# Where the even and odd tokens are told apart: in the split of the MLP activations, or in the weight load of the up-projection

## The chip, the cores and the metric

The program runs on one core of a Trainium2 chip. The metric is device microseconds of one execution. Beside the time there is a profile of one execution: for each engine the start and duration of its instructions, and what it waited for. TensorE appears twice in it, as PE (the matmuls) and as PEld (the loads of the stationary operand, which run beside the matmuls).

## The reference, cut to what matters

Two decoder layers act on 256 tokens of width 2048, all in float32. In each layer four groups of attention heads are followed by an output projection, and then comes the gated MLP, with which this document is concerned:

```
h = rms_norm(x, ffn_norm)                  # 256 x 2048
u = causal_depthwise_conv(h @ w_up, ...)   # w_up: 2048 x 11264, width 3 along the tokens
gate, val = split(u, 2)
x = x + (silu(gate) * val) @ w_down        # w_down: 5632 x 2048
```

## The kernel before

**Precision by three products.** Every float32 operand of the large products is split into a high and a low part in the type float32r (`hi`, `lo`), and the product is made of three matmuls: high by high, low by high, high by low (lines 269, 270 and 271 in `Gemm.steps`). The activations are the stationary operand, 128 rows by 128 tokens; the weights are the moving one, 128 rows by 512 columns. Each of the three matmuls has its own load of the stationary operand, since the operand alternates between high and low.

**Tokens.** The 256 tokens are two halves, `t` = 0 and 1, each with an accumulator in PSUM of 128 partitions by 512 columns. For most products half `t` holds tokens 128t to 128t + 127. The up-projection is different: half 0 holds the even tokens and half 1 the odd ones. What follows it (`turn`, line 845 and after) transposes 32 by 32 blocks of the two halves, interleaves them in pairs, and writes them to DRAM and back, so that the channels come to lie on the partitions and the tokens in order along the row, as the convolution needs them.

**How the order is made before.** `x_ready` transposes the residual `xs` in blocks of 128 by 128 on TensorE (line 208, tiles `tr_f` ahead of the MLP and `tr_n` ahead of the next layer) and splits each 128 by 256 block into `hTs` with `split_T`: ScalarE writes the high part (line 190), VectorE the low part (line 191). For the MLP, `even_odd` makes these two instructions read the PSUM block with a step of two elements, and `halves` names the halves of the written row. So `hTs` holds 128 even tokens and then 128 odd ones, and the stationary operand of `up` is 128 neighbouring elements per partition, as for every other product. `hTs` has for each of the 16 row blocks `k` a row of 256 float32r elements for the high part and another for the low part.

**Order of the work.** The loop over the up-projection makes 11 pairs of a gate product and a value product of 512 columns in each layer, in three groups of 3, 4 and 4, each followed by its part of the down-projection. The weights come by DMA from the SyncE queue, 1 MB at a time, and ScalarE and VectorE split them (lines 242 and 243). Side work (transposes, convolution, splits) is put between the matmul steps by a queue of generators (`Task`, `tick`). The order of instructions on each engine is fixed when the program is built. The attention part has products with fewer columns and products in plain float32, which the program issues as two TensorE instructions each.

Of the kernel before, what the change touches and what calls it, by code (L numbers as in the profile page):

```python
# [19 lines left out]
P = 128  # L20
NT = 2
SEQ = 256
DM = 2048
KT = DM // P
# [50 lines left out]
def tile_trunk(ctx: ExitStack, tc: tile.TileContext, x, xT, pvec, rows, ctab,  # L75
# [35 lines left out]
    class Task:  # L111
        def __init__(self, gen, q=queue):
            self.gen, self.done = gen, False
            q.append(self)
# [4 lines left out]
    def tick(n=1):  # L119
        for _ in range(n):  # L120
            for task in [*movers, *list(queue)[:1]]:
                with tc.issue_after(last_mm[0].ins):
                    try:
                        next(task.gen)
                    except StopIteration:
                        task.done = True
                        (movers if task in movers else queue).remove(task)
# [19 lines left out]
    def pcol(l, n, i=0):  # L147
        o = l * PVW + PV[n] + i
        return pv[:, o:o + 1]
# [14 lines left out]
    hTs = big.tile([P, KT, 2, SEQ], F32R, name="hTs")  # L164
# [8 lines left out]
    def psum(name):  # L173
        return trp.tile([P, 512], F32, tag="tr", name=name)
# [14 lines left out]
    def split_T(src, gain, hi, lo):  # L189
        nc.scalar.activation(hi, src, AF.Identity, scale=gain)  # L190
        nc.vector.scalar_tensor_tensor(lo, src, gain, hi.bitcast(F32), op0=ALU.mult, op1=ALU.subtract)

    def even_odd(a):

        return a.rearrange("p (m t) -> p t m", t=NT)

    def halves(a):
        return a.rearrange("p (t m) -> p t m", t=NT)

    def transpose_split(src, n, cnt, gain, kt0, dh, dl, eo=False):  # L200

        for j0 in range(0, cnt, 2):
            if j0:
                yield
            ps = psum(f"tr_{n}_{j0}")
            for j in (j0, j0 + 1):
                for t in range(NT):
                    nc.tensor.transpose(ps[:, (j - j0) * SEQ + t * P:(j - j0) * SEQ + (t + 1) * P],
                                        src[:, t, j * P:(j + 1) * P], ident)
            for j in (j0, j0 + 1):  # L210
                a, h, lo = ps[:, (j - j0) * SEQ:(j - j0 + 1) * SEQ], dh[:, kt0 + j, :], dl[:, kt0 + j, :]
                if eo:
                    a, h, lo = even_odd(a), halves(h), halves(lo)
                split_T(a, gain(j), h, lo)

    def acc_bank(name):
        return accp.tile([P, 512], F32, tag="acc", name=name)
# [8 lines left out]
    def split_weights(src, k, N, n, nk):  # L226


        if k % 4 == 0 and (n, k) not in loaded:
            load_weights(src, k, n, nk)  # L230
        raw = loaded[n, k - k % 4][:, k % 4:k % 4 + 2]
        if n == "dq0" and k == 0:
            src(raw, 0, 1, nc.scalar)
            src(raw[:, 1:], 1, 1)
        elif n == "dq0" and k < 8:
            src(raw, k, 2)
        hi, lo = [], []
        for s in ((0, 1), (1, 2)) if n == "dq0" and k == 0 else ((0, 2),):
            r = raw[:, s[0]:s[1], :N]
            h, w = (wspl.tile([P, 2, 512], F32R, tag=p, name=f"{p}_{n}_{k + s[0]}")[:, :s[1] - s[0], :N]  # L240
                    for p in ("hi", "lo"))
            nc.scalar.copy(h, r)  # L242
            nc.vector.tensor_tensor(w, r, h.bitcast(F32), op=ALU.subtract)  # L243
            hi += [h[:, i] for i in range(s[1] - s[0])]
            lo += [w[:, i] for i in range(s[1] - s[0])]
        return hi, lo

    class Gemm:


        def __init__(self, n, N, act, wsrc, nk, bank=acc_bank):
            self.n, self.N, self.act, self.wsrc, self.nk = n, N, act, wsrc, nk
            self.acc = [bank(f"acc_{n}_{t}") for t in range(NT)]
            self.done = 0

        def steps(self, k0, cnt):
            N = self.N
            for g0 in range(k0, k0 + cnt, 2):
                hi, lo = split_weights(self.wsrc, g0, N, self.n, self.nk)
                parts = [(*self.act(g0 + i), hi[i], lo[i]) for i in range(2)]  # L260
                order = [(t, i) for t in range(NT) for i in range(2)]
                if self.n == "dq0" and g0 == 0:
                    order = [(t, i) for i in range(2) for t in range(NT)]
                for t, i in order:
                    o = self.acc[t][:, :N]
                    ah, al, wh, wl_ = parts[i]
                    first, last = self.done + i == 0, self.done + i == self.nk - 1
                    sh, sl = ah[:, t * P:(t + 1) * P], al[:, t * P:(t + 1) * P]
                    nc.tensor.matmul(o, sh, wh, start=first, stop=False)  # L269
                    nc.tensor.matmul(o, sl, wh, start=False, stop=False)  # L270
                    last_mm[0] = nc.tensor.matmul(o, sh, wl_, start=False, stop=last)  # L271
                self.done += 2
                tick(rate[0])
# [5 lines left out]
    def wchunk(w, k0=0):  # L279

        def src(raw, k, cnt, q=nc.sync):
            q.dma_start(raw[:, :cnt, :w.shape[2]], w[:, k0 + k:k0 + k + cnt, :])
        return src
# [7 lines left out]
    def slotted(slots, tasks):  # L291
        def get(k):
            finish(tasks[k // 4])
            hi, lo = slots[k // 4]
            return hi[:, k % 4, :], lo[:, k % 4, :]
        return get

    def evac(acc, n, N, rs, tag, bufs):
        d = tmp.tile([P, NT, 512], F32, tag=tag, name=f"{tag}_{n}", bufs=bufs)
        for t in range(NT):  # L300
            nc.scalar.activation(d[:, t, :N], acc[t][:, :N], AF.Identity, scale=rs[:, t:t + 1])
        return d
# [12 lines left out]
    def x_ready(c, n, gname, l, ssq, r, reo=None):  # L315

        yield from transpose_split(xs[:, :, c * 512:(c + 1) * 512], f"{n}_{c}", 4,
                                   lambda j: pcol(l, gname, 4 * c + j), 4 * c, hTs[:, :, 0], hTs[:, :, 1],
                                   reo is not None)
        yield  # L320
        yield from x_stats(c, n, ssq, r, reo)

    def x_stats(c, n, ssq, r, reo=None):
        for t in range(NT):
            tc.keep_in_program_order(sumsq(xs[:, t, c * 512:(c + 1) * 512], f"{n}_{c}_{t}", ssq[:, t, c:c + 1]))
        if c == 3:
            yield
            s = sml.tile([P, NT], F32, tag="xs_s", name=f"s_{n}")
            nc.vector.tensor_reduce(s, ssq, axis=AX.X, op=ALU.add)
            if n[0] == "n":  # L330
                with tc.issue_after(tc.keep_in_program_order(nc.scalar.preload_act_table_set(LNEXP)).ins):
                    rsqrt(r, s, f"x{n}", 1.0 / DM, NT)
            else:
                rsqrt(r, s, f"x{n}", 1.0 / DM, NT)
            if reo is not None:
                rd = dram.tile([SEQ], F32, tag="rd", name=f"rd_{n}")
                nc.gpsimd.dma_start(rd.rearrange("(t p) -> p t", p=P), r)
                nc.gpsimd.dma_start(reo, rd.rearrange("(p t) -> p t", t=NT))
# [137 lines left out]
    for l in range(L):  # L476
# [46 lines left out]
        def cq_task(l=l):  # L523
            for t in range(NT):
                sumsq(cq[:, t, :], f"cq{l}_{t}", ss_lat[:, 2 + t:3 + t])
            rsqrt(r_lat[:, 2:4], ss_lat[:, 2:4], f"cq{l}", 1.0 / QR, 2)
            yield from transpose_split(cq, f"cq{l}", 4, lambda j: pcol(l, "cq", j), 0, *cqT)
# [3 lines left out]
        acc = lat_gemm.acc  # L531
# [72 lines left out]
        for c, (c0, wu) in enumerate(((0, w_uqn[l]), (GW, w_uqr[l]))):  # L604
            w = wu.shape[2]
            acc = Gemm(f"uq{l}_{c}", w, slotted([cqT], [t_cq]), wchunk(wu), 4).run()
# [4 lines left out]
        for c in range(2):  # L611
            acc = Gemm(f"ukv{l}_{c}", 512, slotted([ckvT], [t_lat]), wchunk(w_ukv[l, c]), 2).run()
# [217 lines left out]
        reo = sml.tile([P, NT], F32, tag="reo", name=f"reo_{l}", bufs=1)  # L830

        def post_out(c, acc):
            add_x(c, acc)
            h_task[c] = Task(x_ready(c, f"f{l}", "ffn", l, ssq_x, rf, reo))
# [21 lines left out]

        def up(n, j):

            acc = Gemm(f"up_{n}", 512, hT, wchunk(w_up[l, j]), KT).run()
            u = evac(acc, n, 512, reo, "v", 1)  # L860
            d = tmp.tile([P, 4, SEQ], F32, tag="qk", name=f"u_{n}", bufs=2)
            gen = turn(u, d, n)
            next(gen)
            return d, Task(gen, movers)
# [39 lines left out]
        for ti, (j0, j1) in enumerate(THIRDS):  # L904
            act, tasks = [], []
# [23 lines left out]
            nk = (j1 - j0) * 4  # L929
# [74 lines left out]
```

## Time and profile before

| | |
|---|---|
| median of 3 runs | 2226.51 us (2224.54 to 2228.56) |
| the profiled execution | 2224.77 us, of which the span from first to last instruction is 2222.6 us |
| PE busy | 2215.8 us, 10196 matmuls |
| PEld busy | 1839.2 us, 10196 loads |
| VectorE, ScalarE busy | 1452.1 us, 1192.0 us |
| granted TensorE clock, mean | 0.999 of full speed |

[...] The rate is read from the distance of one start to the next.

### The profile page before, as it was taken

To read this page: it belongs to the slowest core of one execution; us is meant where nothing else is said; L and a number is where in the kernel's file an instruction comes from. 1 tells how busy PE (TensorE), PEld (TensorE's weight loads), DVE (VectorE), ACT (ScalarE), POOL (GpSimd) and SP (SyncE) were. 2 spreads that over 40 slices of the span, in tenths; PEclk is the share of its full clock that TensorE was granted. 3 is DMA by queue.
4 is the path that set the end of the run, shared out by engine and by line. 5 is a ranking of instruction groups with operands and counts; after the bars stand their busy time and mean duration, and the time that the engine had idled before them with its cause. 6 is when DMAs were issued, how large, how long until landed. Compare 5 with 4: busy or idle time off the path is not lost.

```text
span 2222.6 us, 27073 instructions
## 1 busy us (share of the span) xinstructions
PE 2215.8 (100%) x10196; PEld 1839.2 (83%) x10196; DVE 1452.1 (65%) x2071; ACT 1192.0 (54%) x1651; POOL 3.9 (0%) x11
## 2 busy tenths in 40 slices
PE   9999999999999999999999999999999999999999
PEld 8888888888888888888888888888888888888887
DVE  6865865667566664667568658665766676656664
ACT  7555545555446553555556555455554555435552
POOL 0000000000000000000000000000000000000000
PEclk9999999999999999999999999999999999999999
DMA  8535445777677865777555444457775778658774
GB/s 323 199 133 171 155 156 185 216 238 242 212 213 242 252 217 195 235 238 234 183 171 195 146 155 168 152 190 220 234 245 199 230 237 243 212 197 243 232 234 150
DMA packets 163988, 460.84 MB, mean 207 GB/s; under 512 B 100496, under 2 KB 106000, under 8 KB 115728
## 3 DMA queue, kind: packets, MB, share of 16 engines
q1 hardware_dynamic: 63744, 411.63, 55.0%
q10 hardware_dynamic: 99984, 47.46, 9.3%
q8 instruction: 80, 1.31, 0.2%
q14 instruction: 52, 0.43, 0.1%
q0 software_dynamic: 128, 0.00, 0.0%
HBM read 433.89 MB, written 25.17 MB: 207 GB/s over the span
## 4 chain that ended last, share of the span: by engine, by line
PE 99%; DVE 0%; DMA 0%; ACT 0%; issue 0%; SPq 0%; DVEq 0%; ACTq 0%
PE acc_dn L270 7%; PE acc_dn L269 7%; PE acc_up_g L271 7%; PE acc_dn L271 7%; PE acc_up_g L269 7%; PE acc_up_v L269 7%; PE acc_up_g L270 7%; PE acc_up_v L270 7%; PE acc_up_v L271 7%; PE acc_out L271 3%; PE acc_out L269 3%; PE acc_out L270 3%; PE acc_aq L269 1%; PE acc_bk L271 1%; PE acc_av L269 1%; PE acc_bk L269 1%
## 5 line engine op out<-in xcount | busy, mean ns | idle before, releaser
L243 DVE TENSOR_TENSOR lo_dn<-raw_dn,hi_dn 128x1024 fp32r<-128x1024 f32 x176 | 214.9, 1224 | 163.6 <-ACT hi_dn L242 163.6
L243 DVE TENSOR_TENSOR lo_up_g<-raw_up_g,hi_up_g 128x1024 fp32r<-128x1024 f32 x176 | 213.1, 1220 | 163.4 <-ACT hi_up_g L242 163.4
L242 ACT CAST hi_dn<-raw_dn 128x1024 fp32r<-128x1024 f32 x176 | 185.8, 1056 | 230.0 <-PE acc_dn L270 200.8
L242 ACT CAST hi_up_g<-raw_up_g 128x1024 fp32r<-128x1024 f32 x176 | 185.2, 1055 | 201.4 <-PE acc_up_v L270 66.4
L243 DVE TENSOR_TENSOR lo_up_v<-raw_up_v,hi_up_v 128x1024 fp32r<-128x1024 f32 x176 | 213.6, 1223 | 117.0 <-ACT hi_up_v L242 117.0
L242 ACT CAST hi_up_v<-raw_up_v 128x1024 fp32r<-128x1024 f32 x176 | 185.1, 1053 | 184.3 <-PE acc_up_v L270 80.9
L269 PE MATMUL acc_up_g<-hi_up_g,hTs 128*128 128x512 f32 x704 | 274.2, 390 | 0.0
L271 PE MATMUL acc_up_g<-lo_up_g,hTs 128*128 128x512 f32 x704 | 273.9, 389 | 0.0
L270 PE MATMUL acc_up_g<-hi_up_g,hTs 128*128 128x512 f32 x704 | 273.9, 389 | 0.0
L269 PE MATMUL acc_up_v<-hi_up_v,hTs 128*128 128x512 f32 x704 | 273.9, 389 | 0.0
L270 PE MATMUL acc_up_v<-hi_up_v,hTs 128*128 128x512 f32 x704 | 273.9, 389 | 0.0
L271 PE MATMUL acc_up_v<-lo_up_v,hTs 128*128 128x512 f32 x704 | 273.9, 389 | 0.0
L271 PEld LDWEIGHTS acc_up_g<-lo_up_g,hTs 128*128 128x128 f32 x704 | 132.2, 188 | 27.5
L271 PEld LDWEIGHTS acc_up_v<-lo_up_v,hTs 128*128 128x128 f32 x704 | 132.2, 188 | 27.5
L269 PEld LDWEIGHTS acc_up_v<-hi_up_v,hTs 128*128 128x128 f32 x704 | 132.2, 188 | 27.4
L270 PEld LDWEIGHTS acc_up_v<-hi_up_v,hTs 128*128 128x128 f32 x704 | 132.2, 188 | 27.4
L270 PEld LDWEIGHTS acc_up_g<-hi_up_g,hTs 128*128 128x128 f32 x704 | 132.2, 188 | 27.3
L269 PEld LDWEIGHTS acc_up_g<-hi_up_g,hTs 128*128 128x128 f32 x704 | 132.2, 188 | 27.3
L243 DVE TENSOR_TENSOR lo_out<-raw_out,hi_out 128x1024 fp32r<-128x1024 f32 x64 | 78.3, 1224 | 57.0 <-ACT hi_out L242 54.1
L242 ACT CAST hi_out<-raw_out 128x1024 fp32r<-128x1024 f32 x64 | 67.3, 1051 | 63.0 <-PE acc_out L270 46.5
L269 PE MATMUL acc_dn<-hi_dn,a0h_f 128*128 128x512 f32 x192 | 74.9, 390 | 0.0
L269 PE MATMUL acc_dn<-hi_dn,a1h_f 128*128 128x512 f32 x192 | 74.8, 389 | 0.0
(576 smaller groups left out, 4535.7 us busy)
## 6 DMA issues: line engine op xcount, KB each, us to landing
raw_up_g<-in_w_up_dram SPq DMA_DIRECT2D x88, 1024.0 KB, 5.2
raw_up_v<-in_w_up_dram SPq DMA_DIRECT2D x88, 1024.0 KB, 5.2
raw_dn<-in_w_down_dram SPq DMA_DIRECT2D x88, 1024.0 KB, 4.9
raw_out<-in_w_out_dram SPq DMA_DIRECT2D x32, 1024.0 KB, 4.8
td_g<-T_g ACTq DMA_DIRECT2D x22, 512.0 KB, 2.6
u_g<-td_g ACTq DMA_DIRECT2D x88, 128.0 KB, 6.0
td_v<-T_v ACTq DMA_DIRECT2D x22, 512.0 KB, 2.8
u_v<-td_v ACTq DMA_DIRECT2D x88, 128.0 KB, 5.8
```

The lines of the kernel that those rows point to most:

```text
L242: nc.scalar.copy(h, r)
L243: nc.vector.tensor_tensor(w, r, h.bitcast(F32), op=ALU.subtract)
L269: nc.tensor.matmul(o, sh, wh, start=first, stop=False)
L270: nc.tensor.matmul(o, sl, wh, start=False, stop=False)
L271: last_mm[0] = nc.tensor.matmul(o, sh, wl_, start=False, stop=last)
```

## The change

The split of the MLP activations writes `hTs` in token order, with both operands read and written in sequence, as for the other products. `Gemm` has a new flag `eo`, which only `up` sets. With it, the stationary operand of half `t` is the columns t, t + 2, t + 4, ... of the 256: 128 elements per partition, 8 bytes apart. What each accumulator receives is the same as before. No instruction is added, removed or moved; the access patterns of the splits and of the up-projection's weight loads are others.

```
-                a, h, lo = ps[:, (j - j0) * SEQ:(j - j0 + 1) * SEQ], dh[:, kt0 + j, :], dl[:, kt0 + j, :]
-                if eo:
-                    a, h, lo = even_odd(a), halves(h), halves(lo)
-                split_T(a, gain(j), h, lo)
+                split_T(ps[:, (j - j0) * SEQ:(j - j0 + 1) * SEQ], gain(j), dh[:, kt0 + j, :], dl[:, kt0 + j, :])
...
-        def __init__(self, n, N, act, wsrc, nk, bank=acc_bank):
+        def __init__(self, n, N, act, wsrc, nk, bank=acc_bank, eo=False):
+            self.eo = eo
...
-                    sh, sl = ah[:, t * P:(t + 1) * P], al[:, t * P:(t + 1) * P]
+                    cols = slice(t, SEQ, NT) if self.eo else slice(t * P, (t + 1) * P)
+                    sh, sl = ah[:, cols], al[:, cols]
...
-            acc = Gemm(f"up_{n}", 512, hT, wchunk(w_up[l, j]), KT).run()
+            acc = Gemm(f"up_{n}", 512, hT, wchunk(w_up[l, j]), KT, eo=True).run()
```

## Rows read from the trace of the kernel before

**Rows 1.** The page: busy time, share of the span and instructions of each engine.
```profile
PE 2215.8 (100%) x10196; PEld 1839.2 (83%) x10196; DVE 1452.1 (65%) x2071; ACT 1192.0 (54%) x1651; POOL 3.9 (0%) x11
```

**Rows 2.** The page: chain that ended last, share of the span by engine.
```profile
PE 99%; DVE 0%; DMA 0%; ACT 0%; issue 0%; SPq 0%; DVEq 0%; ACTq 0%
```

**Rows 3.** Waits of PE (all three) and the longest of PEld: total us, times, longest.
```profile
PE wps L105 <- DVE warm L102: 1.1, 1, 1.1
PE acc_dq L269 <- ACT hi_dq L242: 0.5, 1, 0.5
PE tr_yc L208 <- DVE y_c L432: 0.4, 2, 0.2
...
PEld pT_a L404 <- ACT lg_a L396: 2.3, 8, 0.4
```

**Rows 4.** Stretch of up-projection: us, busy PE, PEld, DVE, ACT, POOL; PEclk, DMA, GB/s.
```profile
420.00:540.00 120.00, 120.00 (x531) 99.41 (x530) 79.13 (x102) 68.27 (x84) 0.00 (x0) 1.00 0.81 251
```

**Rows 5.** Groups by form: up-projection matmuls and loads, count | busy, mean ns | idle.
```profile
L270 PE MATMUL acc_up_g<-hi_up_g,hTs 128*128 128x512 f32 x704 | 273.9, 389 | 0.0
...
L270 PEld LDWEIGHTS acc_up_g<-hi_up_g,hTs 128*128 128x128 f32 x704 | 132.2, 188 | 27.3
```

**Rows 6.** Timeline of the up-projection: start us, duration us, instruction.
```profile
391.58 0.39 PE L269 MATMUL acc_up_g<-hi_up_g,hTs 128*128 128x512 f32 x1
391.58 0.19 PEld L270 LDWEIGHTS acc_up_g<-hi_up_g,hTs 128*128 128x128 f32 x1
391.81 0.39 PE L270 MATMUL acc_up_g<-hi_up_g,hTs 128*128 128x512 f32 x1
391.81 0.19 PEld L271 LDWEIGHTS acc_up_g<-lo_up_g,hTs 128*128 128x128 f32 x1
...
393.62 0.39 PE L269 MATMUL acc_up_g<-hi_up_g,hTs 128*128 128x512 f32 x1
```

**Rows 7.** Timeline, float32r products with 256 columns, first and last of 18 matmuls.
```profile
73.93 0.28 PE L269 MATMUL acc_uq<-hi_uq,a0h_cq 128*128 128x256 f32 x1
...
75.97 0.28 PE L271 MATMUL acc_uq<-lo_uq,a0h_cq 128*128 128x256 f32 x1
```

**Rows 8.** Timeline, float32r products with 324 columns, first and last of 13 matmuls.
```profile
29.92 0.31 PE L269 MATMUL acc_lat<-hi_lat,hTs 128*128 128x324 f32 x1
...
31.71 0.32 PE L269 MATMUL acc_lat<-hi_lat,hTs 128*128 128x324 f32 x1
```

**Rows 9.** Timeline, plain float32 products with 128 and 256 columns, and 4 columns.
```profile
110.56 0.38 PE L418 MATMUL s_d<-dT_d 128*128 128x128 f32 x2
110.78 0.39 PE L418 MATMUL s_d<-dTr_d,qz 128*128 128x128 f32 x2
111.00 0.60 PE L420 MATMUL s_d<-dT_d 128*128 128x256 f32 x2
111.44 0.59 PE L420 MATMUL s_d<-dTr_d,qz 128*128 128x256 f32 x2
111.87 0.27 PE L645 MATMUL qk_d<-ident,a2l_dq 128*128 128x128 f32 x1
...
58.14 0.36 PE L561 MATMUL cum<-fz,ct 128*128 128x4 f32 x2
58.36 0.36 PE L562 MATMUL cum<-fz,ct 128*128 128x4 f32 x2
58.59 0.48 PE L269 MATMUL acc_aq<-hi_aq,hTs 128*128 128x512 f32 x1
```

**Rows 10.** The splits by line: duration ns min/median/max, first and last start us.
```profile
L190 ACT ACTIVATE hTs<-tr_f,pv x32: 463/474/477, 343.4 to 1507.5; 128x256 fp32r<-128x256 f32 x32
L190 ACT ACTIVATE hTs<-tr_n,pv x16: 456/470/477, 1081.6 to 1122.2; 128x256 fp32r<-128x256 f32 x16
...
L191 DVE SCALAR_TENSOR_TENSOR hTs<-tr_f,pv,hTs x32: 476/482/489, 344.7 to 1508.0; 128x256 fp32r<-128x256 f32 x32
L191 DVE SCALAR_TENSOR_TENSOR hTs<-tr_n,pv,hTs x16: 477/482/485, 1082.9 to 1122.7; 128x256 fp32r<-128x256 f32 x16
```

More of the change, by code (lines that the diff above doesn't have):

```diff
@@ L191, in split_T, with transpose_split @@
         nc.vector.scalar_tensor_tensor(lo, src, gain, hi.bitcast(F32), op0=ALU.mult, op1=ALU.subtract)
[L193 to L200, printed above, removed]
+    def transpose_split(src, n, cnt, gain, kt0, dh, dl):
         for j0 in range(0, cnt, 2):
@@ L317, in x_ready @@
         yield from transpose_split(xs[:, :, c * 512:(c + 1) * 512], f"{n}_{c}", 4,
-                                   lambda j: pcol(l, gname, 4 * c + j), 4 * c, hTs[:, :, 0], hTs[:, :, 1],
-                                   reo is not None)
+                                   lambda j: pcol(l, gname, 4 * c + j), 4 * c, hTs[:, :, 0], hTs[:, :, 1])
         yield
```

## Prediction, made before the change was run

> **What bounds the kernel now.** I read the page first. TensorE's matmuls cover the whole span and VectorE and ScalarE about 65% and 54% of it [rows 1]; the chain of work that ended last is 99% matmuls [rows 2]. The list of waits confirms it: PE waited three times for anything, 2.0 us in all, and its weight loads at most 2.3 us for any one cause; no wait belongs to the up-projection or to `hTs` [rows 3]. So only what alters the distance from one matmul to the next can alter the time by much. [...]
>
> Then the timeline, for the rate. Line 269 starts at 391.58 and, nine matmuls later, at 393.62: 2.04 us / 9 = 226.7 ns from one to the next [rows 6]. The same timeline shows the load: the load for the next matmul starts when the current matmul starts, and lasts 188 ns in the record, so that about 39 ns of each turn have no load in them (27.3 us idle / 704) [rows 5, 6]. The reader should see two things that run side by side in each turn, the stream of 512 columns and the load of 128 for the next turn; the later of them sets the turn.
>
> **What the change removes.** The step of two in the reads of PSUM: 32 splits on ScalarE and 32 on VectorE. The same instruction on tiles of the same shape without that step is in the trace, ahead of the next layer. ScalarE takes 474 ns with the step and 470 without, VectorE 482 and 482 [rows 10]. That is 32 x 4 ns = 0.13 us on ScalarE, on an engine with half its time free and with no wait of PE behind it: worth 0. If the cover were gone it would be the 0.13 us. The number of instructions, transposes, DMAs and waits stays; nothing moves past a queue.
>
> **What it adds.** A step of two, 8 bytes, in the stationary operand of every up-projection matmul. There are six groups of 704 (three lines, gate and value) [rows 5], 4224 in all, and 4224 x 226.7 ns = 957.6 us, 43% of the time. One nanosecond per matmul is 4.2 us or 0.19%. No load in the trace has a step, so its cost must be bounded.
>
> First, how long does a load without a step occupy TensorE? The 188 ns of the record contain a latency that overlaps: where a product has only 4 columns, four pairs of load and matmul start from 58.14 to 58.59, 0.45 / 4 = 112 ns each [rows 9]. The columns are then next to nothing and the load sets the turn. For float32r the shortest turn in the trace is at 256 columns: 17 turns from 73.93 to 75.97, 120.0 ns [rows 7]. So the load takes about 112 ns and at most 120.
>
> Second, what does the stream take? Between 256 and 512 columns the turn grows from 120.0 to 226.7 ns: 106.7 / 256 = 0.417 ns per column, one cycle of 2.4 GHz. What is left is the same at both: 120.0 - 256 x 0.417 = 13.3 ns per matmul. The 324-column product agrees, with 1.79 us / 12 = 149.2 ns against 135.0 + 13.3 = 148.3 [rows 8]. In the up-projection the stream therefore sets the turn, and a load may grow from 112 or 120 ns to about 227 before it is late: by a factor of 1.9 to 2.0.
>
> Estimate of the added cost, from below and from above:
> - Load as fast as without a step, or slower by up to 1.9: hidden behind the stream, 0.
> - Load of twice 112 ns: 224 ns, still 0. Twice 120 ns: 240 ns, 13.3 ns more per turn than 226.7, 4224 x 13.3 = 56 us. This is the upper end that I use.
> - The far bound from rows: a load that can't run beside the stream at all, 4224 x 112 = 473 us. Nothing in the trace is near that; I keep it as a tail only.
> - Below nothing: the plain float32 products leave less over than float32r: 217.5 ns at 256 columns (0.87 us / 4) and 110 at 128 (0.44 / 4), so 0.84 ns per column and 110 - 107.5 = 2.5 ns [rows 9]. If the 13.3 ns belonged to how a dense float32r operand is loaded and a stepped one were loaded in the plain way, each turn would lose 10.8 ns: 4224 x 10.8 = 46 us.
>
> I take 0. The row nearest to a stepped load is that of the dense load, and it would have to become 1.9 times as long before anything is seen. ScalarE's and VectorE's reads at the same step of 8 bytes cost nothing in [rows 10], though there from PSUM and at a slower pace, so this is a weak hint.
>
> [...]
>
> **Sum.** Profiled execution 2224.77 us, of which 2222.6 us is the span and 2.2 us lies around it; minus 0.13 us that is hidden; plus 0: about 2225. The profiled execution lies 1.7 us below the median of the three runs shown, 2226.51, whose spread is 4 us. I give 2226.
>
> **Rivals.**
> - *The stationary read disturbs the moving stream (slower).* Place: the 13.3 ns that each float32r matmul takes beyond its columns. [...] A dense load covers 128 x 4 = 512 bytes per partition; with the step it spans 1024. If the excess is what the load takes from the stream and it goes with the length of the span, it doubles: 13.3 x 4224 = 56 us, 2281 us. For it: the excess is fixed per matmul, as a load is. Against it: a fixed cost of float32r that has nothing to do with the load would look the same. It decides from about 1 ns per matmul on, since there is no slack in the stream. [...] The late load of 240 ns has the same price.
> - *The load becomes far longer (slower by more).* At three times 112 ns the turn would be 336 ns, 109 ns more: 461 us, 2686 us. For it speaks only that no stepped load is on record; against it, the step is small. About 5 in 100.
> - *The excess of float32r goes (faster).* 46 us less, 2179 us, as worked out above. It needs a load path that depends on the step, and nothing in the trace shows one.
> - *The change does nothing to the loads but alters the order of instructions* because the program is built with other operand ranges: PE's waits are 2.0 us in all, so this is worth a microsecond or two either way, inside no change.
>
> **How the numbers follow.** About 0.2% of the time, 4.5 us, is what a measurement can tell from no change. Forecast, load hidden and stream undisturbed: 0.62. Slower: 0.33, of which 0.21 at up to 56 us (either mechanism, fully or in part), 0.07 between that and the tail, 0.05 in the tail. Faster: 0.05. Hence faster 0.05, same 0.62, slower 0.33. For 8 in 10 the range must take in the 56 us: from 2221 (4 us under the lowest run) to 2286 (the 2281 of the first rival and the spread of the runs). The forecast's own range is 2222 to 2231.
>
> **What would show it.** In the changed kernel line 269 of the up-projection should again start every 226.7 ns, PE's span from the first to the last of such a run be unchanged, and the splits take 470 and 482 ns. If the recorded load grows from 188 ns but the distance stays, the load was hidden. A distance of 240 ns would show the first rival or the late load; which of the two, only a product with fewer columns tells: with a late load the turn would not shrink with the columns, with a disturbed stream it would. A distance near 217 ns would be the faster rival. Other engines can't make the forecast wrong by much: in the up-projection they have a third of their time free [rows 4].

## The result, and the profile after

The changed kernel takes 2252.85 us (2252.72 to 2253.34, four runs) against 2225.8 us: a ratio of 1.0124, 95% interval 1.0112 to 1.0137, or 27 us slower. No change was forecast, at 2226; the range reached to 2286 and held the time.

The page of the changed kernel, its busy times; TensorE's matmuls still cover the span, and nothing else grew by more than 3 us against [rows 1] but the loads, by 22:
```profile
PE 2244.0 (100%) x10196; PEld 1861.3 (83%) x10196; DVE 1455.1 (65%) x2071; ACT 1190.9 (53%) x1651; POOL 3.8 (0%) x11
```

Its waits of PE, in four lines where [rows 3] had three; together 2.4 us, none in the up-projection:
```profile
PE wps L105 <- DVE warm L102: 1.1, 1, 1.1
PE acc_dq L261 <- ACT hi_dq L232: 0.6, 2, 0.4
PE tr_yc L201 <- DVE y_c L423: 0.4, 2, 0.2
PE acc_dq L263 <- DVE lo_dq L233: 0.3, 1, 0.3
```

Its stretch of up-projection, in the columns of [rows 4]: 516 matmuls in 120 us where there were 531, at the same granted clock of 1.00. Beside it the groups of [rows 5]:
```profile
420.00:540.00 120.00, 120.00 (x516) 99.27 (x515) 77.95 (x102) 67.14 (x81) 0.00 (x0) 1.00 0.78 241
```
```profile
L262 PE MATMUL acc_up_g<-hi_up_g,hTs 128*128 128x512 f32 x704 | 277.4, 394 | 0.0
...
L262 PEld LDWEIGHTS acc_up_g<-hi_up_g,hTs 128*128 128x128 f32 x704 | 135.9, 193 | 28.2
```

And its timeline, for the rate, as in [rows 6]. Each matmul lasts 0.39 us in the record and the next starts about 0.23 us after it, so they overlap and the distance of the starts is the turn; the two matmuls shown are twelve turns apart:
```profile
480.14 0.39 PE L263 MATMUL acc_up_v<-lo_up_v,hTs 128*128 128x512 f32 x1
480.14 0.19 PEld L261 LDWEIGHTS acc_up_v<-hi_up_v,hTs 128*128 128x128 f32 x1
480.38 0.19 PEld L262 LDWEIGHTS acc_up_v<-hi_up_v,hTs 128*128 128x128 f32 x1
...
482.94 0.39 PE L263 MATMUL acc_up_g<-lo_up_g,hTs 128*128 128x512 f32 x1
```

2.80 us / 12 = 233.3 ns per turn, against 226.7. So 6.6 ns x 4224 = 28 us: this is nearly the whole difference of the spans, 2251.1 - 2222.6 = 28.5 us. The order of the instructions is the same on every engine. The reader should see what doesn't fit a late load: the recorded load grew by only 5 ns, and about 40 ns of each turn still have none (28.2 us / 704). The splits run as before: 472 ns on ScalarE with the step gone (474 in [rows 10]), 480 on VectorE (482).

### The profile page after: what moved, and what is told of

Read it like the earlier page. It is cut to its first block, busy times and chain, and to the rows that moved or that the text cites. A ratio compares the mean times of both kernels' runs of the same rounds, so it can differ in the third digit from the quotient of the medians.

```text
span 2251.1 us, 27073 instructions
## 1 busy us (share of the span) xinstructions
PE 2244.0 (100%) x10196; PEld 1861.3 (83%) x10196; DVE 1455.1 (65%) x2071; ACT 1190.9 (53%) x1651; POOL 3.8 (0%) x11
## 4 chain that ended last, share of the span: by engine, by line
PE 99%; DVE 0%; DMA 0%; ACT 0%; issue 0%; SPq 0%; DVEq 0%; ACTq 0%
PE acc_up_g L261 7%; PE acc_up_v L261 7%; PE acc_up_g L263 7%; PE acc_up_g L262 7%; PE acc_up_v L262 7%; PE acc_up_v L263 7%; PE acc_dn L261 7%; PE acc_dn L263 7%; PE acc_dn L262 7%; PE acc_out L263 2%; PE acc_out L261 2%; PE acc_out L262 2%; PE acc_aq L261 1%; PE acc_bk L263 1%; PE acc_cq L263 1%; PE acc_bk L261 1%
## 5 line engine op out<-in xcount | busy, mean ns | idle before, releaser
L232 ACT CAST hi_dn<-raw_dn 128x1024 fp32r<-128x1024 f32 x176 | 185.4, 1053 | 231.0 <-PE acc_dn L262 200.5
L261 PE MATMUL acc_up_g<-hi_up_g,hTs 128*128 128x512 f32 x704 | 277.8, 395 | 0.0
L262 PE MATMUL acc_up_g<-hi_up_g,hTs 128*128 128x512 f32 x704 | 277.4, 394 | 0.0
L261 PE MATMUL acc_up_v<-hi_up_v,hTs 128*128 128x512 f32 x704 | 277.4, 394 | 0.0
L262 PE MATMUL acc_up_v<-hi_up_v,hTs 128*128 128x512 f32 x704 | 277.4, 394 | 0.0
L262 PEld LDWEIGHTS acc_up_v<-hi_up_v,hTs 128*128 128x128 f32 x704 | 135.9, 193 | 28.4
L261 PEld LDWEIGHTS acc_up_v<-hi_up_v,hTs 128*128 128x128 f32 x704 | 135.9, 193 | 28.3
L261 PEld LDWEIGHTS acc_up_g<-hi_up_g,hTs 128*128 128x128 f32 x704 | 135.9, 193 | 28.2
L262 PEld LDWEIGHTS acc_up_g<-hi_up_g,hTs 128*128 128x128 f32 x704 | 135.9, 193 | 28.2
```

## The experiments

**Which part costs.** Two kernels with one part of the change each. In the first the split stays as it was, in even and odd tokens, and only the load gets the step:
```
-                    sh, sl = ah[:, t * P:(t + 1) * P], al[:, t * P:(t + 1) * P]
+                    cols = slice(t, SEQ, NT) if self.n[:2] == 'up' else slice(t * P, (t + 1) * P)
+                    sh, sl = ah[:, cols], al[:, cols]
```


> The kernel before, with its split into even and odd tokens kept, and only the step of two put into the up-projection's weight loads; so the tokens of the MLP reach the accumulators in another order and the output leaves the right order out. Theory A or B (the loads cost all of it): 2252 to 2254 us, 233.3 ns from matmul to matmul in the up-projection. Rival (the split in token order is what costs, through the engines that feed TensorE): 2224 to 2228 us.

In the second the change is made and only the step taken out again:
```
-            acc = Gemm(f"up_{n}", 512, hT, wchunk(w_up[l, j]), KT, eo=True).run()
+            acc = Gemm(f"up_{n}", 512, hT, wchunk(w_up[l, j]), KT).run()
```


> The changed kernel with the step taken out of the weight loads: the split writes token order, the up-projection reads 128 neighbouring tokens, and the order of the tokens behind it is left out. Theory A or B: 2224 to 2228 us as before the change, 226.7 ns from matmul to matmul. Rival (the split costs): 2252 us.

Measured: 2252.78 us (ratio 1.0124, 1.0109 to 1.0139) and 2225.01 us (1.000, 0.9991 to 1.0009). The loads cost all of it, the splits nothing.

**A load that is late, or a stream that is disturbed?** A kernel that runs nothing but rows of 60 equal matmuls, back to back:
```
s, m = ops[n][:, 0, :], ops[n][:, 1, :]
...
base = off + (i % 2) * 1024
a = s[:, base:base + step * (P - 1) + 1:step]
nc.tensor.matmul(p[:, :N], a, m[:, 0:N], start=i == 0, stop=i == cnt - 1)
```


> This kernel leaves the whole computation out (it writes x back) and measures the load by itself: runs of 60 matmuls whose stationary operand is 128 elements with a step of 1, 2, 3, 4 or 8, with 512, 384, 256, 128 and 32 moving columns in float32r, and some in plain float32 and bfloat16. What is read is the distance from one matmul to the next. All theories: 226.7 ns for step 1 at 512 columns, 120 at 256. Theory A (the stepped load takes time from the moving stream, or adds a fixed piece to each turn): about 233.3 ns for step 2 at 512 columns, and the same 6.6 ns on top at 384 and 256 columns (180, 127). Theory B (the load itself becomes long and is late): about 233 ns at step 2 whatever the columns, 512, 384 or 256, and at 32 columns too. Within A: if the cost goes with the span of bytes that is read, step 3 costs 13 and step 4 costs 20 ns more than step 1; if it is the same for any step, 6.6 ns for all. An odd first element makes no difference in either.

Its timeline, the first matmul of some of the rows; each row is 60 matmuls long, so the distance to the next row's first, over 60, is the turn. In the names, "two" is the step, and a, b, c, d are 512, 384, 256 and 128 columns:
```profile
39.58 0.39 PE L40 MATMUL r_two_a<-sr 128*128 128x512 f32 x1
53.58 0.39 PE L40 MATMUL r_twoodd_a<-sr 128*128 128x512 f32 x1
67.58 0.40 PE L40 MATMUL r_three_a<-sr 128*128 128x512 f32 x1
81.71 0.40 PE L40 MATMUL r_four_a<-sr 128*128 128x512 f32 x1
95.81 0.41 PE L40 MATMUL r_eight_a<-sr 128*128 128x512 f32 x1
...
110.53 0.33 PE L40 MATMUL r_one_b<-sr 128*128 128x384 f32 x1
120.95 0.34 PE L40 MATMUL r_two_b<-sr 128*128 128x384 f32 x1
131.35 0.40 PE L40 MATMUL r_four_b<-sr 128*128 128x384 f32 x1
145.35 0.28 PE L40 MATMUL r_one_c<-sr 128*128 128x256 f32 x1
152.54 0.28 PE L40 MATMUL r_two_c<-sr 128*128 128x256 f32 x1
159.74 0.39 PE L40 MATMUL r_four_c<-sr 128*128 128x256 f32 x1
173.74 0.22 PE L40 MATMUL r_one_d<-sr 128*128 128x128 f32 x1
180.39 0.28 PE L40 MATMUL r_two_d<-sr 128*128 128x128 f32 x1
187.45 0.39 PE L40 MATMUL r_four_d<-sr 128*128 128x128 f32 x1
```

| turn, ns | 512 columns | 384 | 256 | 128 |
|---|---|---|---|---|
| step 1 | 226.7 (mean from the eleventh start on) | 173.7 | 119.8 | 110.8 |
| step 2 | 233.3 | 173.3 | 120.0 | 117.7 |
| step 4 | 235.0 | 233.3 | 233.3 | 233.6 (see below) |

Both theories fall. At 384 and 256 columns the step of two costs nothing, so there is no fixed piece per turn (theory A) and no load of 230 ns (theory B). At 128 columns the load sets the turn: 111 ns without a step, 118 with a step of two, where 128 columns at 0.417 ns are 53. The step of four shows what a late load looks like: 233 ns at 384 and 256 columns alike. Theory A's price by the span falls too: steps of three and eight took 235.5 and 245.3 ns at 512 columns, where 13 ns more had been expected for three and 20 for four. Thus the load of the changed kernel takes about 118 ns (an estimate, from the row with 128 columns), far from late, and still the turn at 512 columns is 6.6 ns longer. (The granted clock was 1.00 from 180.39 to 187.45 us, the row of step two and 128 columns, and 0.50 from 201.47 to 214.23; it fell within the row of step four between them, and the rows with 32 columns behind it are left aside.) In bfloat16 no cost was seen at 512 columns: 216 ns without a step, 215.8 at steps of two, four and eight.

The load alone moved the turn at 512 columns from 226.7 to 233.3 ns without being late; so the running matmuls are not free of it.

**The same in the whole kernel.** A step of four, over the high and the low row of `hTs` together, and the halving of the columns, with dense and with stepped loads:
```
+            row = hTs[:, k, :, :].rearrange("p a s -> p (a s)")
+            return row[:, t:2 * SEQ:4], row[:, t + 2:2 * SEQ:4]
...
+                    for c in (slice(0, 256), slice(256, 512)) if self.n[:2] == "up" else (slice(0, N),):
+                        nc.tensor.matmul(o[:, c], sh, wh[:, c], start=first and not c.start, stop=False)
```


> The changed kernel with a step of four in the up-projection's loads, taken from the high and the low row of hTs together, so the product is of mixed-up operands: the right tokens and parts are left out. The first probe's row for step 4: the load sets the turn at 233.3 ns for 384, 256 and 128 columns, and at 512 columns the turn is 235.0. If that holds in the kernel, 226.7 becomes 235.0: 2224.8 + 4224 x 8.3 ns = 2260 us. Theory A as first put, cost by the span of bytes read: three times 6.6 ns, 2309 us.

> The kernel before, each up-projection matmul made as two of 256 columns, each with its own load. 8448 turns of 120.0 ns instead of 4224 of 226.7: 56 us more, 2281 us.

> The changed kernel with the same halving to 256 columns. If the step costs nothing at 256 columns, as in the first probe, the same 2281 us as with dense loads. If every stepped load costs its 6.6 ns, 8448 x 6.6 ns = 56 us more: 2337 us.

Measured: 2260.44 us (ratio 1.0159, 1.0144 to 1.0174), 2280.67 (1.025, 1.0235 to 1.0266) and 2280.94 (1.0251, 1.0234 to 1.0268). All three as the rows of the probe said. A load of twice the length (233 ns against 118 in the probe) costs only 8 us more than the change, and 8448 stepped loads at 256 columns cost no more than dense ones.

**One stepped load in three.**
```
-                    sh, sl = ah[:, cols], al[:, cols]
+                    sh, sl = ah[:, t * P:(t + 1) * P], al[:, cols]
```


> The changed kernel with the step kept only in the load of the low part, one of the three loads of each product (1408 of 4224); the token order is left out for the other two. If each stepped load costs by itself, a third of the 27 us: 2234 to 2236 us, and only the turn in which the stepped load runs, or the one behind it, grows by 6.6 ns. If it is a state of the engine that one stepped load brings on, more than a third: up to 2252 us.

Measured: 2243.46 us (1.0081, 1.0065 to 1.0098), 19 us and not 9. A third of the loads brings two thirds of the loss; the price isn't one per stepped load.

**More columns.** The second probe, in rows of 48:

> The computation is left out again (x is written back); runs of 48 float32r matmuls. The first probe gave, for step 1 and step 2: 226.7 and 233.3 ns at 512 columns, 173.4 and 173.4 at 384, 120.0 and 120.0 at 256. So neither a fixed piece per turn nor a late load fits, and the columns between 384 and 512 are to tell where the 6.6 ns come in. Theory C (the stepped load takes something from the stream only when the stream is long): a gradual rise, about half at 448 columns. [...] Further: with the same stationary block again and again, with two accumulator banks in turn, or with single products (start and stop in each), step 1 stays at 226.7 unless the 13.3 ns beyond the columns come from one of these; a product with 64 stationary columns tells whether the 13.3 and the 6.6 go with the length of the load (then 6.7 and 3.3). Of mixed steps, one stepped load in three is expected at 231.1 on average, as the kernel with the low part stepped had it (2243.5 us), and one in two between 230 and 233.3.

Two rows of its timeline with 448 columns and the start of the next; over 48 that is 206.5 ns dense and 203.3 stepped:
```profile
90.54 0.36 PE L43 MATMUL one_cx<-sr 128*128 128x448 f32 x1
100.45 0.37 PE L43 MATMUL two_cx<-sr 128*128 128x448 f32 x1
110.21 0.35 PE L43 MATMUL one_dx<-sr 128*128 128x416 f32 x1
```

All of it, as mean distance from the eleventh to the forty-seventh start, and what is left beyond 0.4167 ns per column:

| columns | 512 | 496 | 480 | 448 | 416 | 400 | 320 |
|---|---|---|---|---|---|---|---|
| dense, ns | 226.7 | 220.0 | 216.7 | 206.7 | 186.7 | 180.0 | 146.7 |
| beyond the columns | 13.4 | 13.3 | 16.7 | 20.0 | 13.4 | 13.3 | 13.4 |
| step 2, ns | 233.3 | 225.2 | 220.0 | 203.3 | 186.7 | 180.0 | 146.7 |
| beyond the columns | 20.0 | 18.5 | 20.0 | 16.6 | 13.4 | 13.3 | 13.4 |

Not C: at 448 columns the stepped load is the faster one. Nor is it a matter of 512 columns alone: at 496 the step costs 5.2 ns. All of these means but 225.2 lie on multiples of 6.67 ns (16 columns' worth, at 0.4167 ns each) or of half of it: 180.0 is 27 of them, 186.7 is 28, 203.3 is 30.5, 226.7 is 34, 233.3 is 35. Two accumulators in turn and the same block again and again left 226.7 and 233.3 as they were; single products, tried with dense loads alone, left 226.7. Below the table's columns the load sets the turn (111.7 ns dense at 224 and at 192 columns alike), and there the step does cost: 120.0 ns at 224. A dense load that started 8 bytes further on took 230.6. Of 64 stationary columns the dense load took 230.0 and the stepped one 226.7. One stepped load in three gave 231.1, as in the kernel above (2243.46 us, by 4224 x 4.4 ns = 19 us); one in two gave 230.2, so the cost doesn't simply grow with their number.

**Where the load starts.** So the next suspect, theory E in what follows, was how the reads of load and stream fall against each other: where each of them starts. The probe shifts the start of the load, and then that of the stream.

> The computation is left out (x is written back); runs of 40 float32r matmuls with 512 columns, if not said otherwise. The second probe showed turns that sit on a grid of 6.67 ns or on a half or third of it (226.7, 220.0, 206.7, 233.3, 230.0), and a dense load that starts 8 bytes off at 230.6. [...] If some start gives less than 226.7, there is something to gain for the whole kernel.

The timeline of dense loads in rows of 40; they start 12 (c), 16 (d), 256 (i) and 512 bytes (j) further on:
```profile
53.16 0.40 PE L42 MATMUL soff_c<-sr 128*128 128x512 f32 x1
62.37 0.40 PE L42 MATMUL soff_d<-sr 128*128 128x512 f32 x1
71.70 0.39 PE L42 MATMUL soff_e<-sr 128*128 128x512 f32 x1
...
108.98 0.39 PE L42 MATMUL soff_i<-sr 128*128 128x512 f32 x1
118.05 0.39 PE L42 MATMUL soff_j<-sr 128*128 128x512 f32 x1
127.11 0.40 PE L42 MATMUL moff_a<-sr 128*128 128x512 f32 x1
```

230.3 ns (c), 233.3 (d), and 226.8 and 226.5 at 256 and 512 bytes. Theory A, cost by the span that the load reads, is out: the shifted loads span the same 512 bytes. With the stream left where it was, the start of the load counts, as theory E has it: an offset of 16, 32 or 64 bytes costs 6.6 to 6.7 ns, and one of 128 bytes 5.7; of those tried only 256 and 512 are free. For the stream likewise: 229.0 to 236.7 ns for offsets of 4 to 128 bytes, 226.7 from 256 on. Loads of 32 to 124 columns lay between 226.7 and 233.3 without order. No start gave less than 226.6.

The same probe has six more counts of columns, among them 504, dense and then stepped:
```profile
385.77 0.38 PE L42 MATMUL none_b<-sr 128*128 128x504 f32 x1
394.84 0.39 PE L42 MATMUL ntwo_b<-sr 128*128 128x504 f32 x1
403.91 0.38 PE L42 MATMUL none_c<-sr 128*128 128x500 f32 x1
```

9.07 / 40 = 226.75 ns for both. At 508 and 500 columns the step costs nothing either, nor at 472 (213.3 and 213.4); at 464 it costs 2.8 ns and at 432 it saves 2.1. So the cost of the step comes and goes with the count: 6.6 ns at 512, none at 504 (where dense loads run no faster than at 512), 5.2 at 496, 3.3 at 480, none at 472.

In the kernel before, dense loads that start 8 bytes off; they take tokens 2 to 129 and 126 to 253 in place of 0 to 127 and 128 to 255, so the right tokens are left out:
```
+                    off = t * P + ((2, -2)[t] if self.n[:2] == "up" else 0)
+                    sh, sl = ah[:, off:off + P], al[:, off:off + P]
```


> [...] Theory E: as in the second probe, 230.6 ns per turn instead of 226.7, 4224 x 3.9 = 16 us more: 2241 us. [...]

Measured: 2248.29 us (ratio 1.010, 1.0084 to 1.0117), 23 us and more than the 16 forecast: dense loads at a step of one cost nearly what the step of two costs. The trace has 232.2 ns per turn, 5.5 ns more than before: 231.0 in half 0, whose load starts 8 bytes further on, and 233.5 in half 1, whose load starts 8 bytes earlier, a start that no probe had.

**Can a stepped load run at 226.7?**

> The computation is left out (x is written back); runs of 32 float32r matmuls with 512 columns. The third probe had dense loads at 230 to 233 ns wherever they started less than 256 bytes off, and at 226.7 at 256 and 512 bytes, and the same for the start of the stream. Theory E (the fall of the reads against each other decides, and 226.7 is its best case): stepped loads, too, come to 226.7 or less than 230 ns for some of the 60 combinations of where load and stream start, and the rest scatters between 228 and 236; dense loads get worse or better only with the difference of the two starts. Theory F (a stepped load costs its 6.6 ns or a good part of it wherever it starts): no combination of the 60 lies under 230 ns.

The timeline of rows of 32 stepped loads, with the load 32 bytes on and the stream 0 (a) and 16 bytes on (b):
```profile
100.35 0.39 PE L42 MATMUL two_ca<-sr 128*128 128x512 f32 x1
107.78 0.39 PE L42 MATMUL two_cb<-sr 128*128 128x512 f32 x1
115.04 0.39 PE L42 MATMUL two_cc<-sr 128*128 128x512 f32 x1
```

7.43 / 32 = 232.2 and 7.26 / 32 = 226.9 ns. Of the 60 combinations the mean was 232.3, and only this one ran at 226.7; six were at 230.0 to 230.1. The values for a load 256, 512 and 768 bytes on repeat those for 0. So theory F is out by one case in 60.

The same probe has twelve rows of dense loads; in three of them the load starts 128 bytes on and the stream 64 (a), 128 (b) and 256 (c):
```profile
516.02 0.39 PE L42 MATMUL one_ca<-sr 128*128 128x512 f32 x1
523.49 0.39 PE L42 MATMUL one_cb<-sr 128*128 128x512 f32 x1
530.76 0.40 PE L42 MATMUL one_cc<-sr 128*128 128x512 f32 x1
538.22 0.39 PE L42 MATMUL one_da<-sr 128*128 128x512 f32 x1
```

233.4, 227.2 (226.7 once it has settled, from the eleventh start on) and 233.1 ns. What counts for dense loads is thus above all the difference of the two starts, and not where the load starts: in all four rows in which this difference is a multiple of 256 bytes the turn settled at 226.7, also with both 64 or 128 bytes on; the other eight lay at 228.9 to 233.6. For stepped loads the difference decides in the same way as long as both starts are multiples of 64 bytes (233.3 ns at none, 230.0 at 64 bytes, 231.4 at 128). Elsewhere it doesn't: a load 96 bytes on took 230.0 with the stream at 0 and 233.3 with the stream at 256 bytes, and a difference of 16 bytes gave 233.3 twice and 226.7 once.

The case of 226.7 in the complete kernel:
```
+    hTp = big.tile([P, KT * 2 * SEQ + 64], F32R, name="hTs")
+    hTs, hTm = (hTp[:, o:o + KT * 2 * SEQ].rearrange("p (k a s) -> p k a s", a=2, s=SEQ) for o in (0, 8))
...
+            off = 4 if n[:2] == "up" else 0
+            h, w = (wspl.tile([P, 1088], F32R, tag=p, name=f"{p}_{n}_{k + s[0]}")[:, off:off + 1024]
```


> The changed kernel, complete, with the stepped loads kept, but the MLP's activations start 32 bytes further on in hTs and the up-projection's weights 16 bytes further on in their tiles: the one combination of 60 that ran at 226.7 ns in the probe (the 256-byte pads take the place of the warm-up's own tile, which now borrows another zeroed one). Half 0 of the tokens starts at exactly that place, half 1 one element later, which no probe has. Theory E (the starts decide): half 0 at 226.7 ns, half 1 between 226.7 and 236, so between 2225 and 2245 us, and under the 2252.9 of the change. Theory F (the step has a price of its own): 2252 to 2254 us, 233.3 ns as in the change.

Measured: 2244.07 us (ratio 1.0087, 1.007 to 1.0103); 9 of the 27 us come back. The time lies in the range expected, but not for the reason given: the two halves of the tokens don't differ. The trace shows two rhythms, one after the other. First two stretches in the columns of [rows 4], in the first and the second group of the up-projection:
```profile
420.00:540.00 120.00, 120.00 (x531) 103.22 (x531) 79.29 (x102) 67.39 (x83) 0.00 (x0) 1.00 0.83 249
640.00:760.00 120.00, 120.00 (x516) 100.24 (x515) 80.28 (x106) 66.50 (x82) 0.00 (x0) 1.00 0.78 237
```

531 matmuls in 120 us as in the kernel before, and then 516 as after the change, with the same line, tiles, step and start. Of the six groups the two that follow the output projection begin at 226.7 ns, and the four that follow a down-projection run at 233.3. In the second layer the change from one to the other can be seen in the timeline:
```profile
1601.67 0.39 PE L263 MATMUL acc_up_g<-hi_up_g,hTs 128*128 128x512 f32 x1
...
1602.35 0.39 PE L263 MATMUL acc_up_g<-hi_up_g,hTs 128*128 128x512 f32 x1
1603.10 0.50 PE L264 MATMUL acc_up_g<-lo_up_g,hTs 128*128 128x512 f32 x1 [0.36 <-DVE lo_up_g L234]
1603.44 0.39 PE L262 MATMUL acc_up_g<-hi_up_g,hTs 128*128 128x512 f32 x1
...
1606.94 0.40 PE L262 MATMUL acc_up_g<-hi_up_g,hTs 128*128 128x512 f32 x1
```

Three turns take 0.68 us before the matmul at 1603.10 (226.7 ns); that one waits once for VectorE; the fifteen after 1603.44 take 3.50 us (233.3 ns), and it stays so to the end of the stretch. In all, 1082 of the 4224 turns ran at 226.7 ns in this execution of 2246.53 us. The other three took 2243.9 to 2244.1 us, 2.5 us less. That is about what this wait and the 262 turns behind it cost (an estimate: 0.5 us + 262 x 6.6 ns = 2.2 us), so those executions may have had no such wait; they have no trace.

## Why the prediction was wrong

- *What bounds the kernel* was right: PE's chain alone, no wait in the up-projection, and only the distance from matmul to matmul moved the time. (PE's waits in [rows 3] are four, in three lines; the 2.0 us are right.)
- *The splits are worth 0* was right (2225.01 us with that part alone).
- *The load is hidden up to a factor of 1.9, so the step costs 0* is the step that failed. Its first half holds: the stepped load takes about 118 ns in place of 111 (the turns at 128 columns), not the 224 to 240 that the prediction also allowed for, and is never late; even at 233 ns, with a step of four, it costs only 8.3 ns of turn. But I took the 13.3 ns beyond the columns for a constant, because they were the same at 256, 324 and 512 columns of [rows 6 to 8]. They are the smallest value of any float32r row here, and all three rows happen to show it; the changed kernel has 20.0 ns, 6.6 x 4224 = 28 us. (The 2.4 GHz of the prediction is 1 / 0.417 ns, the pace of the columns in [rows 6, 7]; the traces give the clock as a share of full speed only, and no run shows what a cycle is.) The trace of the kernel before held a sign of this that I passed over, in dense loads of the output projection, behind other products and then further on:
```profile
319.19 0.39 PE L271 MATMUL acc_out<-lo_out,a3h_d 128*128 128x512 f32 x1
...
320.81 0.39 PE L269 MATMUL acc_out<-hi_out,a3h_d 128*128 128x512 f32 x1
...
329.11 0.39 PE L270 MATMUL acc_out<-hi_out,a1l_b 128*128 128x512 f32 x1
...
333.19 0.39 PE L270 MATMUL acc_out<-hi_out,a1l_b 128*128 128x512 f32 x1
```
  The first seven turns take 1.62 us (231.4 ns each), the later eighteen 4.08 us (226.7).
- *The first rival*, a disturbed stream, named the right place, the excess over the columns, and the right sign; its mechanism, a cost by the span that the load reads, is refuted (nothing at 256 columns, 120.0 ns against 119.8; 23 us for a dense load 8 bytes off; a step of four no dearer than one of three), and its price of 56 us was twice the measured one. The chance of 0.21 for "up to 56 us, fully or in part" is where the time fell. That the range held the time is luck in so far as its upper end came from this refuted mechanism and from a late load that wasn't late.
- *What only fewer columns can tell* was rightly named as the test, and it excluded both of my mechanisms.

What the runs support in their place: at 512 columns of float32r the turn depended on load and stream together. Dense loads in rows ran at 226.7 ns where their start differed from that of the stream by a multiple of 256 bytes, the others tried at 228.9 to 236.7, and the step of two, at 233.3, turned the best case into an ordinary one. That it is their reads that meet well or badly is my reading; no trace shows the reads. That load and stream together decide, and not the load's length or step by itself, is shown by the dense rows, in which the difference of the starts counted and not the load's start alone, and by one kernel in which the same line on the same tiles ran at 226.7 and, after a wait, at 233.3 ns. What inside the engine has such a rhythm, why many means settle on the 6.67 ns grid, and what chooses the rhythm after a pause is not shown. A pause alone isn't enough: the six groups of the changed kernel each began behind other products and all ran at 233.3, those of the kernel before at 226.7, and with one stepped load in three two turns of 0.59 and 0.90 us (waits of 0.2 and 0.5 us, between 420 and 540 us) left the 231.1 as it was (605 turns in 139.83 us from 640.14 on). No version with changed loads beat the kernel before.

## What to carry to other kernels

A load hidden by its length wasn't free here: at about 118 ns in a turn of 226.7 it made the turn 6.6 ns longer. So where the stream sets the turn with no slack, test the access pattern of the stationary operand itself, by the distance between matmul starts, at the column count that the kernel uses. In the float32r rows of the probes a step of two was free at 256, 320, 384, 400, 416 and 504 columns and cost 3% of a turn at 512 (233.3 ns against 226.7); a dense operand whose start didn't differ from that of the stream by a multiple of 256 bytes cost 1 to 4% (228.9 to 236.7 ns). In bfloat16 the step was free at 512 columns (215.8 ns against 216). If a permutation can be had for nothing in another engine's access pattern, as in the split before this change (ratio 1.000 with the split alone changed), leave it there.

## What had not been expected of the hardware

- In the rows of float32r matmuls whose stream set the turn, the turn had 13.3 ns beyond its columns at the least; at 512 columns most other starts and steps gave 15 to 23 (226.7 against 228.9 to 236.7 ns), the changed kernel 20.0.
- Dense loads in rows at 512 columns ran at 226.7 ns when the starts of load and stream differed by a multiple of 256 bytes, whatever the starts themselves (0, 64, 128 and 256 bytes on).
- The same line on the same tiles ran in two lasting rhythms, 226.7 and 233.3 ns, in one kernel (`stepped_shifted_starts`), and there it went from one to the other at a single wait.
- A step of four doubled the load (233 ns against 111 to 118), yet cost only 8.3 ns per turn at 512 columns (235.0), where the turn without it took 226.7 ns anyway.
